# A fused decoder block in 16-bit-split fp32: another written-out order of its mixer and gate stage, and fixed places for the mixer's tiles

## Chip, cores and metric

The kernel runs on one core of a Trainium2 chip, as one launch. The metric is device time in microseconds (us), the median of three runs. The engines are TensorE (PE; its weight loads are PEld), VectorE (DVE), ScalarE (ACT), GpSimd (POOL) and SyncE (SP), which issues DMAs.

## What is computed

512 tokens and 16 prepended meta tokens, width 1024, one layer, everything in fp32. Cut to what matters:

```python
proj = rms_norm(h, norm1_g) @ w_in                      # q 512, k 128, v 128, u 512
attn = sliding_window_attention(q, k, v, ...)           # 8 heads, window 128, sinks, meta tokens
ssm  = s5_ssm(u, ...)                                   # 32 groups x 64 complex states, GLU
h    = h + concat(rms_norm(attn), rms_norm(ssm)) @ w_out
tok  = rms_norm(h, norm2_g)                             # 512 x 1024
q    = tok @ w_query                                    # 8 heads x 2 halves x 128
s1, s2 = q_half1 @ keys1, q_half2 @ keys2               # 128 keys each
v1, i1 = top_k(s1, 16); v2, i2 = top_k(s2, 16)
sc, ci = top_k(v1[:, None] + v2[None], 16)              # 16 of 256 sums
idx  = i1[ci // 16] * 128 + i2[ci % 16]                 # of 16384 experts
g    = softmax(sc)
act  = gelu(peer_u[idx] . tok) * g
h    = h + sum(act * peer_v[idx])                       # 16 experts x 8 heads per token
```

## The kernel before

Every fp32 operand of a large product is split into a high part (cast or scaled on ACT, L94 and L97) and a low part (what is left, a subtraction, L95 and L98); a product is three matmuls, high·high, low·high and high·low.

**Mixer** (`front`). Its 498 steps stand in the string `STEPS`, and the code runs them in that order, so that the string is each engine's order. `lw` loads a weight tile (L229), `lx` a pair of x tiles (L220), `sx`/`su` split them, `u0` to `u7` are the eight steps of 24 matmuls that form the 512 SSM channels (L184 to L186, into all eight PSUM banks `ps_u`); each needs the two parts of one x tile (`xh`, `xl`) and one weight tile (`w_uh`, `w_ul`). In between DVE and POOL work out the state-space constants (`tt`, L172; the blocks `bdr`, `bdi` are copied by ACT, L587). At the end the attention and SSM outputs meet in `wo`, the second norm (L971) and its transposes `nt` (L977) give `hTh` and `hTl` (L194), what all later products read.

Nine tiles of 128×2304 fp32 rotate under one tag (`b8`), and eight PSUM banks under another (`ps`): the next tile takes the place that was given out longest ago.

**Gate stage** (in `body`). Its 899 steps stand in `WSTEPS`:

- `Lq`, `Aq`, `Dq` load one of 16 query weight tiles, make its high part on ACT (L1041) and its low part (L1045), on DVE for the numbers in `QV`, else on POOL; `qm`, `qk`, `qs`, `qo` are the product (L1050 to L1052), its evacuation (L1057), the 128 key scores (L1063) and their copy to `qsc` (L1067).
- `tk` finds the 16 best keys of one head half and token tile, with MAX8, FIND_INDEX8 and MATCH_REPLACE8 on DVE (L1016 to L1024); then, per token tile n, `ca`, `tp`, `ga`, `rk`, `xe` and `oh` (one-hot work, L1137 to L1145) turn them into 16 experts per head.
- Gates, for n < 3: `go` and `gg` make one-hot rows (L1187) and weighted ones (`ggt`, L1201) on DVE, `gm` multiplies them on PE (`ps_gm`, L1217, L1218), `gc` copies the result by ACT (L1224), `gs` stores it: a dense table of gates.
- For the first 54 of 128 blocks of experts: `Lu` loads a block of `peer_u` (L1317), `Au` makes its high part `uh` on ACT (L1321), `Du` its low part `ul` (L1325), on DVE for the blocks in `UV`, else on POOL; `sm` is the block's 74 matmuls `ps_sb` with the tokens (L1333 to L1335), `so` its copy `s` by ACT (L1341).
- `rl` and `rs` gather single rows for the fourth token tile, whose experts are not done densely (L1366, L1386).

**Main loop** over 128 blocks (L1483 to L1548): gates times scores, gelu, and the products with `peer_v` (`acc`, L1543 to L1545), beside the scores of the blocks from 54 on and the rows of the fourth tile (L1393).

Of the kernel before, what the change touches and what calls it, by code (L numbers as in the profile page):

```python
# [110 lines left out]
STEPS = """
    bdz Lx4 drz Lwu3 Lwu1 ang Lwu5 Lx0 Swu3 Sx4 Lwu0 Lwu4 Swu1 sin par0 Lprm Swu0 Sx1 Lwu6 Lwq0 par1 Sx0 Swu5 Lwkv3
    Swu6 Lwkv2 par2 Lxn0 Lxm par3 sq1 par4 Lx2 rot0 rot1 Lx6 Lxn2 Sx2 co00 Lwu2 sq0 u0 Lwkv1 u1 Swkv1 Swu2 Swu4 Lwu7
    sq2 co30 rot2 Sx3 u2 u3 Sx5 wt00 wt10 bdc Swkv3 u4 sq3 u5 sq4 Lwkv0 r1 Sx6 Lwo70 rot3 Sx7 Lwq1 Swkv0 u6 Swq0 par5
    Swu7 wt01 u7 uc0 dg2 dg0 dg3 uc3 rm0 dg1 Lwq7 rm2 Swkv2 rm3 rm1 wt11 dg4 we00 co31 co01 rm4 uc1 Lwq6 kv0 we10 rot4
    rbc co11 we01 wc00 kv3 uc2 Lwq5 wc10 uo1 co10 Lwq2 uo3 rot6 rot5 us1 kv1 k0 kvc3 we11 k3 uo0 kv4 uo2 kc0 us2 co21
    wc01 q0 k1 wt20 us0 kv2 us3 wt21 Swq1 kvc0 we21 wt30 co20 wc11 kvc4 kvc1 q1 wt31 ui0 ui1 M0z kc1 we20 we31 we30
    kvc2 Swq2 x0 kc3 hmq wc21 sc20 wc20 wc31 wc30 hkq x2 hks Lwq3 Swq3 q2 sc21 hms sc00 Lwq4 x1 sc01 diz Swq6 Lwo50 q3
    Swq4 k2 sc02 Swq7 kc2 Swq5 sc03 q4 Lcst Lwo60 q5 sc10 hmx Lwo00 sc11 q6 hkx mt kd1 q7 kd0 kt sc22 qc0 qc1 sc12 qc2
    ktc sc13 hq1q hq1s qc3 hq0q y0 hq3q sc23 Lwo01 hq2q hq1x hq2s y1 yc0 y2 hq0s mtc hq3s qt1 hq2x yc1 Lwo71 qtc1 y3  # L120
    ms1 qt2 s11 s10 Lglu yc3 Swo00 yc2 hq0x hq3x msc1 qt0 gelu m11 qtc0 qt3 zt0 zt1 zt2 qtc3 zc0 qtc2 ms0 ms3 ms2 s01
    zc2 zc1 msc2 zt3 s21 m10 zc3 Lg2 sink1 msc0 s20 g0 m21 msc3 m01 s00 m00 e11 pt13 g3 sink0 Lwo20 m20 go0 s31 e10
    e00 pt01 sink2 e01 sums1 go3 g2 sums0 e21 pt02 m31 s30 pmt0 pt11 pmt1 g1 pt23 m30 pt12 Lwo30 pc13 go2 sink3 Swo60
    pt10 pc12 pc11 pc02 Lwo40 Lwo10 gs0 gq0 pmc1 e20 Swo70 pmc0 pm1 pc01 pt00 pm0 pc10 Lwo51 e31 pt32 pc00 pt21 pt20
    pc23 pv12 pt22 pt03 pc32 pc20 pv10 e30 pt31 sums3 pt30 Lwo41 pv00 sums2 pc30 pmt3 go1 pc21 pc03 pmt2 gs2 pmc3 pv02
    Swo71 pmc2 pt33 Swo01 pv01 pm3 pv11 pc22 pv03 pc31 ao0 Swo50 pm2 Lwo61 pc33 Swo40 gs1 gs3 pv30 pv20 pv31 Swo51 gq1
    pv21 Swo61 Swo41 Swo30 at0 as01 pv13 aq0 Lwo31 Swo31 o210 Swo20 ar0 Swo10 Lwo11 o110 Lh1 o211 Swo11 Lwo21 ao1 gq2
    pv22 as00 o011 pv23 gq3 ao2 o000 Swo21 gsum aq2 pv32 pv33 at1 o001 rs aq1 Lh2 oa110 Lh0 as10 ao3 o010 oa011 oa001
    as11 o111 oa210 oa010 oa000 at2 o100 nq01 ar1 as21 oa100 o101 as20 nq00 oa111 nr0 o200 o201 nx00 sh00 nt00 nx01
    at3 oa101 nq11 nq10 sh01 Lh3 ns00 nt01 aq3 o310 nr1 ar2 oa211 as31 ns01 oa201 oa310 nq21 nx10 o311 as30 nt10 ar3  # L130
    nx11 oa200 nq20 nr2 o300 oa311 oa300 nx20 o301 nt11 nt20 ns10 sh10 sh11 nq30 nx21 oa301 ns11 nt21 nq31 nr3 nx30
    nx31 ns21 sh21 ns20 nt30 nt31 sh30 sh31 sh20 ns31 ns30
# [1444 lines left out]
```

## Time and profile before

| | |
|---|---|
| median of 3 runs | 1508.9 us (1508.6 to 1509.43) |
| the profiled execution | 1501.79 us |
| its span, first to last instruction | 1499.9 us, 1.89 us around it |
| mean granted TensorE clock | 0.989 |
| PE busy | 1441.7 us, 96% |
| DVE, ACT, POOL busy | 1172.0 us (78%), 653.4 (44%), 551.9 (37%) |

The mixer takes the span's first 245 us, the gate stage goes on to about 650 us, the main loop to the end. An engine's idle time is shown with what ended it (`<-`): the engine and tile that it waited for. A granted clock of 1.00 is 2.4 GHz, 0.50 is 1.2 GHz.

### The profile page before, as it was taken

Reading aid. Unit: us, or ns where it says so; the run is one execution under the profiler, and the core shown is the slowest. Engines: PE = TensorE matmul, PEld = TensorE weight load, DVE = VectorE, ACT = ScalarE, POOL = GpSimd, SP = SyncE. Lnnn points to the kernel's source line nnn. Section 1 sums busy time; section 2 is a strip of 40 time slices with the busy share of each in tenths; the row PEclk is TensorE's granted clock in tenths of the full one; section 3 lists DMA queues with packets and bytes.
Section 4 is the critical chain, followed back from the end, with each engine's and each line's share of the span. In section 5 each row is a group of like instructions: output and inputs, shape, how many; then the busy total and the mean of one; then the engine's idle time right before and its main releaser. Section 6 shows DMA issues by size and latency. Waiting matters only on the chain. (4 is left out here: it accounts for less than half of the span.)

```text
span 1499.9 us, 22284 instructions
## 1 busy us (share of the span) xinstructions
PE 1441.7 (96%) x8062; PEld 1275.8 (85%) x8062; DVE 1172.0 (78%) x2342; ACT 653.4 (44%) x1189; POOL 551.9 (37%) x392
## 2 busy tenths in 40 slices
...
GB/s 231 84 76 79 50 96 214 95 85 104 135 222 270 262 206 242 289 291 297 330 329 309 352 331 352 328 319 337 300 335 295 345 300 332 331 314 330 311 291 139
DMA packets 161919, 372.79 MB, mean 249 GB/s; under 512 B 19968, under 2 KB 79872, under 8 KB 158608
## 3 DMA queue, kind: packets, MB, share of 16 engines
...
q10 hardware_dynamic: 576, 1.05, 0.2%
q14 instruction: 48, 0.39, 0.1%
...
## 5 line engine op out<-in xcount | busy, mean ns | idle before, releaser
L1333 PE MATMUL ps_sb<-hTh,uh 128*128 128x384 f32 x1024 | 351.9, 344 | 4.9 <-ACT s L1341 4.4
L1335 PE MATMUL ps_sb<-hTh,ul 128*128 128x384 f32 x1024 | 347.0, 339 | 7.9 <-POOL ul L1325 5.1
L1334 PE MATMUL ps_sb<-hTl,uh 128*128 128x384 f32 x1024 | 347.1, 339 | 0.0
L1543 PE MATMUL acc<-vh,ph 128*128 128x512 f32 x768 | 299.7, 390 | 1.3 <-ACT ph L94 1.3
L1544 PE MATMUL acc<-vl,ph 128*128 128x512 f32 x768 | 299.7, 390 | 0.0
L1545 PE MATMUL acc<-vh,pl 128*128 128x512 f32 x768 | 299.2, 390 | 0.0
L1366 POOL DMA_INDIRECT row_grow<-in_v_rows_dram,idx x128 | 180.7, 1412 | 249.2 <-DVE ac L1393 194.0
L1366 POOL DMA_INDIRECT row_grow<-in_u_rows_dram,idx x116 | 161.8, 1394 | 228.3 <-DVE dots L1386 190.3
L1333 PEld LDWEIGHTS ps_sb<-hTh,uh 128*128 128x128 f32 x1024 | 193.7, 189 | 10.7 <-ACT s L1341 7.0
L1335 PEld LDWEIGHTS ps_sb<-hTh,ul 128*128 128x128 f32 x1024 | 193.8, 189 | 10.5 <-POOL ul L1325 6.4
L95 DVE TENSOR_TENSOR vl<-vr,vh 128x1024 fp32r<-128x1024 f32 x128 | 156.8, 1225 | 57.2 <-ACT vh L94 52.9
L1334 PEld LDWEIGHTS ps_sb<-hTl,uh 128*128 128x128 f32 x1024 | 193.6, 189 | 2.8
L1341 ACT ACTIVATE s<-ps_sb 128x384 f32<-128x384 f32 x128 | 63.0, 492 | 275.7 <-PE ps_sb L1335 268.6
L1545 PEld LDWEIGHTS acc<-vh,pl 128*128 128x128 f32 x768 | 144.3, 188 | 31.7 <-DVE pl L95 1.2
L1543 PEld LDWEIGHTS acc<-vh,ph 128*128 128x128 f32 x768 | 144.1, 188 | 30.1 <-ACT ph L94 2.4
L1393 DVE SCALAR_TENSOR_TENSOR ac<-row_grow,dots,ac 128x1024 f32<-128x1024 f32 x128 | 164.2, 1282 | 7.0 <-DMA row_grow<-in_v_rows_dram,idx 5.0
L1544 PEld LDWEIGHTS acc<-vl,ph 128*128 128x128 f32 x768 | 144.2, 188 | 27.0
L1325 DVE TENSOR_TENSOR ul<-ur,uh 128x1024 fp32r<-128x1024 f32 x104 | 127.2, 1224 | 43.0 <-ACT uh L1321 43.0
L94 ACT CAST vh<-vr 128x1024 fp32r<-128x1024 f32 x128 | 134.0, 1047 | 42.5 <-PE acc L1545 36.9
L1321 ACT CAST uh<-ur 128x1024 fp32r<-128x1024 f32 x128 | 133.9, 1047 | 37.2 <-PE ps_sb L1334 16.6
L1386 DVE CUSTOM_DVE_ANT_0 row_grow<-row_grow,hcr 128x1024 f32<-128x1024 f32 x116 | 137.7, 1220 | 3.5 <-DMA row_grow<-in_u_rows_dram,idx 3.5
L94 ACT CAST ph<-s 128x384 fp32r<-128x384 f32 x97 | 49.8, 513 | 186.8 <-DVE s L1498 186.8
...
## 6 DMA issues: line engine op xcount, KB each, us to landing
ur<-in_uT_dram SPq DMA_DIRECT2D x128, 512.0 KB
vr<-in_v_dram SPq DMA_DIRECT2D x128, 512.0 KB
...
```

Of the source, the lines that this page charges most:

```text
L94: nc.scalar.copy(hi, src)
L95: (eng or nc.vector).tensor_tensor(lo, src, hi.bitcast(F32), op=ALU.subtract)
L1321: S.copy(hs[b], ur[b])
L1333: E.matmul(p, hi[:, k], hTh[k][:, :384], start=(k == 0), stop=False)
L1334: E.matmul(p, hi[:, k], hTl[k][:, :384], start=False, stop=False)
L1335: E.matmul(p, lo[:, k], hTh[k][:, :384], start=False, stop=(k == KD - 1))
L1366: nc.gpsimd.indirect_dma_start(out=t, out_offset=None, in_=table, in_offset=bass.IndirectOffsetOnAxis(ap=idx[:, k:k + 1], axis=0))
L1386: V.tensor_tensor_reduce(t, t, hcr, 1.0, 0.0, op0=ALU.mult, op1=ALU.add, accum_out=dots[:, k:k + 1])
L1393: V.scalar_tensor_tensor(ac3, t, dots[:, k:k + 1], ac3, op0=ALU.mult, op1=ALU.add)
L1543: E.matmul(acc[n][h], ph[:, ts], vh[:, cs], start=(b == 0), stop=False)
L1544: E.matmul(acc[n][h], ph[:, ts], vl[:, cs], start=False, stop=False)
L1545: E.matmul(acc[n][h], pl[:, ts], vh[:, cs], start=False, stop=(b == 127))
```

## The change

The two strings hold the same steps, 498 and 899; their order is another one throughout. In the mixer the rotating places become written lists: `B8AT` gives each large tile one of nine places, `PSAT` each PSUM tile one of eight banks. `Pick` keeps its one-hot tiles by half (`self.xe[w]`, `self.oh[w]`), since the steps of the two halves now may interleave. Of the low parts, `QV` gains tile 2, `UV` gains the blocks 1, 3, 9, 14, 18, 21 and 52 and loses 15, 17, 19 and 43. What PE, ACT and the DMAs compute and move is the same. In the changed file a line after about L106 stands 8 further down (9 within `Pick` and `Gates`).

```diff
-NB8 = 9
+B8AT = (
+    "012345678832505230565204517683201"
+)
+PSAT = (
+    "0123456701672301456323415077060726706261047356142730561475230173452617520342601745306125143707356174"
...
-        PP = ctx.enter_context(tc.tile_pool(name="pA", bufs=8, space=PSUM))
+        PP = ctx.enter_context(tc.tile_pool(name="pA", bufs=1, space=PSUM))
+        b8_at, ps_at = iter(B8AT), iter(PSAT)
...
-            return shaped(B8.tile([128, 2304], F32, name=name, tag="b8", bufs=NB8), shape)
+            return shaped(B8.tile([128, 2304], F32, name=name, tag=f"b8{next(b8_at)}"), shape)
...
-            return PP.tile([128, 512], F32, name=name, tag="ps")
+            return PP.tile([128, 512], F32, name=name, tag=f"ps{next(ps_at)}")
...
-        self.xe = self.tile("xe", F16, (128, 8, 16, 16))
+        self.xe[w] = self.tile("xe", F16, (128, 8, 16, 16))
...
-            self.e = self.tile("oh", F16, (128, 8, 16, 16))
+            self.oh[w] = self.tile("oh", F16, (128, 8, 16, 16))
...
-QV = {0, 7}
+QV = {0, 2, 7}
...
-UV = {0, 2, 4, 5, 6, 8, 10, 11, 15, 16, 17, 19, 20, 22, 29, 32, 36, 37, 38, 39, 40, 41, 43, 46, 47, 48, 49, 50, 51, 53}
+UV = {0, 1, 2, 3, 4, 5, 6, 8, 9, 10, 11, 14, 16, 18, 20, 21, 22, 29, 32, 36, 37, 38, 39, 40, 41, 46, 47, 48, 49, 50, 51, 52, 53}
```

Three places of the new order. **The start, on ACT** (a number behind a name tells tiles of one name apart). Before, from the third scaled weight tile on:

```order
L97 ACTIVATE w_uh_193<-w_ur_169,pk 128x512
L94 CAST xh_197<-xr_159 128x528
L94 CAST xh_211<-xr_159 128x528
L97 ACTIVATE w_uh_215<-w_ur_157,pk 128x512
L97 ACTIVATE w_uh_221<-w_ur_201,pk 128x512
L439 ACTIVATE xn_233,ss_85<-xn_233 128x1024
L94 CAST xh_278<-xr_159 128x528
L439 ACTIVATE xn_233,ss_85<-xn_233 128x1024
L97 ACTIVATE w_kvh_349<-w_kvr_323,pk 128x256 x2
L97 ACTIVATE w_uh_355<-w_ur_288,pk 128x512
L97 ACTIVATE w_uh_359<-w_ur_171,pk 128x512
```

and now, from the fifth `u` step's weight tile (w_uh_274) on:

```order
L97 ACTIVATE w_uh_274<-w_ur_165,pk 128x512
L447 ACTIVATE xm,ss_85<-xm 16x1024
L97 ACTIVATE w_uh_279<-w_ur_159,pk 128x512
L94 CAST xh_298<-xr_163 128x528
L94 CAST xh_326<-xr_163 128x528
L447 ACTIVATE xn_228,ss_85<-xn_228 128x1024
L447 ACTIVATE xn_364,ss_85<-xn_364 128x1024
L595 COPY bdr<-prm 64x16x16
L595 COPY bdi<-prm 64x16x16
L595 COPY bdr<-prm 64x16x16
L595 COPY bdi<-prm 64x16x16
L97 ACTIVATE w_uh_398<-w_ur_372,pk 128x512
```

Before, the third `u` step's weight tile (w_uh_355) stood behind two squares of the row norm (L439) and the split of a key weight tile; now the first five `u` steps' weight tiles are made ahead of the row squares, and two squares and the four copies to `bdr` and `bdi` stand ahead of the sixth (w_uh_398) and the seventh.

**The start, on SP**, which issues the loads. Before, from the second pair of x tiles on:

```order
L220 DMA xr_159<-in_xT_dram 128x1056
L229 DMA w_ur_169<-in_w_u_dram 128x512
L229 DMA w_ur_171<-in_w_u_dram 128x512
L314 DMA prm<-in_bc_dram 128x1024
L229 DMA w_ur_201<-in_w_u_dram 128x512
L229 DMA w_qr_203<-in_w_q_dram 128x512
L229 DMA w_kvr_219<-in_w_kv_dram 128x512
L229 DMA w_kvr_225<-in_w_kv_dram 128x512
L430 DMA xn_233<-in_xrow_dram 128x2x1024
L434 DMA xm<-in_xmeta_dram 16x1024
L220 DMA xr_159<-in_xT_dram 128x1056
L220 DMA xr_130<-in_xT_dram 128x1056
```

and now:

```order
L237 DMA w_ur_159<-in_w_u_dram 128x512
L237 DMA w_ur_161<-in_w_u_dram 128x512
L228 DMA xr_163<-in_xT_dram 128x1056
L237 DMA w_ur_165<-in_w_u_dram 128x512
L237 DMA w_ur_167<-in_w_u_dram 128x512
L228 DMA xr_163<-in_xT_dram 128x1056
L442 DMA xm<-in_xmeta_dram 16x1024
```

Two 256 KB weight loads more stand ahead of the pair of x tiles that the first `u` step needs (xr_163), and the third `u` step's tile (w_ur_167) is the eleventh load where it was the 20th (w_ur_288).

**The end of the gate stage, on POOL** (L1325 makes a low part; L1366 gathers rows). Before:

```order
L1325 TENSOR_TENSOR ul_6542<-ur_6359,uh_6448 128x1024
L1366 DMA row_raw<-in_u_rows_dram,idx 128x1024 x2
L1325 TENSOR_TENSOR ul_6892<-ur_6757,uh_6828 128x1024
L1366 DMA row_raw<-in_u_rows_dram,idx 128x1024
L1325 TENSOR_TENSOR ul_6941<-ur_6699,uh_6881 128x1024
L1325 TENSOR_TENSOR ul_6994<-ur_6883,uh_6939 128x1024
L1366 DMA row_raw<-in_u_rows_dram,idx 128x1024
L1325 TENSOR_TENSOR ul_7007<-ur_6924,uh_7005 128x1024
L1366 DMA row_grow<-in_u_rows_dram,idx 128x1024 x4
L1325 TENSOR_TENSOR ul_7070<-ur_7001,uh_7068 128x1024
L1366 DMA row_grow<-in_u_rows_dram,idx 128x1024 x16
```

and now (L1333 and L1374 are the same lines):

```order
L1333 TENSOR_TENSOR ul_6423<-ur_5938,uh_6395 128x1024
L1374 DMA row_raw<-in_u_rows_dram,idx 128x1024
L1333 TENSOR_TENSOR ul_6629<-ur_6406,uh_6606 128x1024
L1374 DMA row_raw<-in_u_rows_dram,idx 128x1024
L1333 TENSOR_TENSOR ul_6788<-ur_6627,uh_6786 128x1024
L1333 TENSOR_TENSOR ul_6866<-ur_6719,uh_6856 128x1024
L1374 DMA row_raw<-in_u_rows_dram,idx 128x1024 x2
L1333 TENSOR_TENSOR ul_6997<-ur_6917,uh_6931 128x1024
L1374 DMA row_raw<-in_u_rows_dram,idx 128x1024
L1374 DMA row_grow<-in_u_rows_dram,idx 128x1024
L1374 DMA row_raw<-in_u_rows_dram,idx 128x1024
L1374 DMA row_grow<-in_u_rows_dram,idx 128x1024 x19
```

Of the low parts, the blocks 21, 9, 18 and 52 have left this list, and 19, 15 and 17 have come in; the last on POOL is that of block 7, which was third from last.

## Rows read from the trace of the kernel before

**Rows 1.** Busy time of each engine in stretches of the span: the stretch in us, its length, busy us of PE, PEld, DVE, ACT and POOL with instructions in brackets, granted TensorE clock, DMA share and GB/s.

```profile
200.00:250.00 50.00, 44.69 (x217) 36.39 (x216) 29.19 (x84) 15.99 (x68) 5.30 (x8) 0.92 0.40 137
...
350.00:400.00 50.00, 43.62 (x232) 41.13 (x231) 47.49 (x245) 26.60 (x30) 16.70 (x7) 0.97 0.39 123
...
450.00:500.00 50.00, 48.01 (x378) 45.96 (x376) 49.32 (x126) 43.00 (x88) 10.21 (x4) 1.00 0.67 242
...
600.00:650.00 50.00, 47.66 (x309) 46.53 (x308) 21.95 (x24) 26.15 (x54) 20.83 (x13) 0.97 0.88 316
...
800.00:1450.00 650.00, 650.00 (x3250) 588.78 (x3250) 525.18 (x630) 227.95 (x316) 282.75 (x208) 1.00 0.92 324
```

**Rows 2.** Waits of PE over the whole span, longest in total first: line, tile, what ended the wait, us in total, times, longest.

```profile
PE ps_u L184 <- ACT xh L94: 13.1, 1, 13.1
PE ps_u L184 <- ACT w_uh L97: 6.5, 1, 6.5
PE ps_sb L1335 <- POOL ul L1325: 5.1, 4, 1.5
PE ps_sb L1333 <- ACT s L1341: 4.4, 6, 1.4
PE ps_xi L535 <- ACT WT L383: 3.0, 1, 3.0
...
PE ps_qq L1050 <- DVE hTl L194: 2.7, 1, 2.7
PE ps_ht L977 <- DVE aux L971: 2.6, 1, 2.6
PE ps_gm L1217 <- DVE ggt L1201: 2.6, 3, 1.3
```

**Rows 3.** Stretches of ten us at the start, with the columns of the first group.

```profile
10.00:20.00 10.00, 5.31 (x22) 5.01 (x23) 8.90 (x32) 3.83 (x8) 6.95 (x14) 1.00 0.89 313
...
30.00:40.00 10.00, 9.64 (x66) 9.33 (x67) 9.55 (x18) 9.30 (x20) 1.85 (x1) 0.82 0.35 103
40.00:50.00 10.00, 10.00 (x84) 9.86 (x82) 6.39 (x13) 2.13 (x6) 9.53 (x11) 1.00 0.27 83
```

**Rows 4.** PE in order of time, 12 to 48 us: start in us, us, engine, line, operation, tiles, count, and in brackets the idle time before.

```profile
15.28 0.59 PE L185 MATMUL ps_u<-xl,w_uh 128*128 128x264 f32 x1 [1.64 <-DVE xl L95]
...
29.85 0.59 PE L184 MATMUL ps_u<-xh,w_uh 128*128 128x264 f32 x1 [6.51 <-ACT w_uh L97]
```

**Rows 5.** PE in order of time, 44 to 56 us: what follows the last `u` step.

```profile
49.45 0.60 PE L457 MATMUL ps_r<-dg,ones 128*128 128x128 f32 x4
```

**Rows 6.** ACT in order of time, 0 to 42 us.

```profile
29.09 1.32 ACT L97 ACTIVATE w_uh<-w_ur,pk 128x512 fp32r<-128x512 f32 x2
...
32.41 0.40 ACT L587 COPY bdr<-prm 64x256 f32<-64x256 f32 x1
```

**Rows 7.** DVE in order of time, 5 to 42 us: of the state-space constants an undisturbed small operation, the first and the last long one of a run, and the last product on `prm`; then low parts of weight tiles.

```profile
18.79 0.17 DVE L172 TENSOR_TENSOR den<-pk 128x16 f32<-128x16 f32 x1
18.99 1.12 DVE L172 TENSOR_TENSOR den<-den,t 128x16 f32<-128x16 f32 x1
...
24.27 1.38 DVE L172 TENSOR_TENSOR t<-nr,pk 128x16 f32<-128x16 f32 x1
...
28.46 0.43 DVE L172 TENSOR_TENSOR prm<-prm 128x256 f32<-128x256 f32 x1
...
29.42 0.88 DVE L98 SCALAR_TENSOR_TENSOR w_kvl<-w_kvr,pk,w_kvh 128x256 fp32r<-128x256 f32 x2
30.21 1.41 DVE L98 SCALAR_TENSOR_TENSOR w_ul<-w_ur,pk,w_uh 128x512 fp32r<-128x512 f32 x2
```

**Rows 8.** POOL in order of time, 0 to 42 us.

```profile
17.22 1.22 POOL L172 TENSOR_TENSOR ptmp<-prm,pr 128x576 f32<-128x576 f32 x1 [1.21 <-issue]
```

**Rows 9.** Waits of DVE, 245 to 560 us.

```profile
DVE wql L1045 <- ACT wqh L1041: 24.7, 1, 24.7
...
DVE v L1016 <- ACT qsc L1067: 4.3, 5, 1.8
```

**Rows 10.** POOL in order of time, 450 to 550 us: low parts of blocks 45, 3 and 13.

```profile
455.68 3.62 POOL L1325 TENSOR_TENSOR ul<-ur,uh 128x1024 fp32r<-128x1024 f32 x1 [3.74 <-ACT uh L1321]
...
516.70 2.54 POOL L1325 TENSOR_TENSOR ul<-ur,uh 128x1024 fp32r<-128x1024 f32 x1 [11.18 <-ACT uh L1321]
541.25 2.71 POOL L1325 TENSOR_TENSOR ul<-ur,uh 128x1024 fp32r<-128x1024 f32 x1 [22.01 <-ACT uh L1321]
```

**Rows 11.** DVE in order of time, 500 to 548 us.

```profile
515.70 4.09 DVE L1201 TENSOR_TENSOR ggt<-goh,g 128x1024 f16<-128x1024 f16 x3
...
523.29 1.28 DVE L1201 TENSOR_TENSOR ggt<-goh,g 128x1024 f16<-128x1024 f16 x2
...
541.02 4.09 DVE L1201 TENSOR_TENSOR ggt<-goh,g 128x1024 f16<-128x1024 f16 x3
```

**Rows 12.** PE in order of time, 505 to 560 us.

```profile
519.84 0.22 PE L1217 MATMUL ps_gm<-ggt,goh 128*128 128x128 f16 x1 [1.12 <-DVE ggt L1201]
```

**Rows 13.** PE in order of time, 540 to 575 us.

```profile
545.16 0.23 PE L1217 MATMUL ps_gm<-ggt,goh 128*128 128x128 f16 x1 [1.27 <-DVE ggt L1201]
```

**Rows 14.** DVE in order of time, 450 to 462 us.

```profile
455.82 1.22 DVE L1325 TENSOR_TENSOR ul<-ur,uh 128x1024 fp32r<-128x1024 f32 x1
```

**Rows 15.** PE in order of time, 640 to 652 us.

```profile
644.64 0.69 PE L1335 MATMUL ps_sb<-hTh,ul 128*128 128x384 f32 x1 [1.52 <-POOL ul L1325]
```

More of the change, by code (lines that the diff above doesn't have):

```diff
@@ L105 @@
 SL = 544
-NB8 = 9
 NRW = 6
 MAGIC = 12582912.0
-STEPS = """
[L112 to L132, printed above, removed]
```

133 lines of the change are left out of this document (78 added, 55 removed).

## The prediction

> **What bounds the kernel now.** I read the stretches of the span first, then PE's waits, then for each stretch with idle PE the engines in order of time. In the stretches [rows 1] PE is busy for all 650 us of 800 to 1450 at a granted clock of 1.00: the main loop is matmuls end to end, the change leaves its code alone, and nothing is to be had there. What PE loses lies ahead of it. Of its longest waits [rows 2] two stand at the start (13.1 us for the first x tile, 6.5 for a weight tile), two at the seam between mixer and gate stage (2.6 and 2.7), 3.0 inside the mixer, and 5.1, 4.4 and 2.6 in the gate stage, for low parts from POOL, copies by ACT and gate rows from DVE. A second loss is the clock: behind a wait it is granted at half for a while, 0.82 on average in 30 to 40 us [rows 3] right behind the wait of 6.51 [rows 4], and 0.92 in 200 to 250 us, 0.97 in 350 to 400 and 600 to 650 [rows 1], stretches that all hold waits. A wait is thus dearer than its row says: 0.03 of 50 us is another 1.5 us.
>
> In the gate stage PE is not its own master. DVE is busy for 47.49 of 50 us in 350 to 400 and 49.32 in 450 to 500 [rows 1], with the searches for the best keys and the one-hot rows. From about 550 us on it is PE that DVE waits for, and DVE has half its time free (21.95 of 50 busy in 600 to 650).
>
> The sum is made against the profiled execution (1501.79 us, of which 1499.9 is span); the median is 7.1 us above it, and I carry differences over to the median unchanged.
>
> **The change, part by part.** No step is added or removed, so PE's busy time stays. The written places and the tiles by half issue no instruction; they only decide which earlier reader a tile waits for, and are counted with the order. That leaves six stretches.
>
> *Start, 0 to 50 us.* Before, the eight `u` steps end at 49.45 [rows 5]; the third waited 6.51 us [rows 4] for a tile that ACT scaled at 29.09 [rows 6], behind two row-norm squares and a pair of key tiles; its load was the 20th. Now this load is the eleventh and the first five steps' tiles are made ahead of the squares, so this wait goes. Two things take its place. Half a MB more is loaded ahead of the first pair of x tiles: at the 313 GB/s of 10 to 20 us [rows 3] that is 1.7 us later, of which the 1.64 us wait for `xl` [rows 4] takes most back, since two x tiles' low parts now stand together. And the sixth step's tile stands on ACT behind the copies to `bdr`, which need DVE's last product on `prm`. That one ended at 28.9 before [rows 7]; ahead of it now stand, by the order of the two kernels, three more x parts and one more weight part (0.70 each) and two key parts (0.44 each) [rows 7], 3.7 us, and x comes 1.7 later: it ends at about 34.3, and four copies of 0.40 and two tiles' worth of 0.66 at most [rows 6] make some 36.5. PE is through five steps (24 matmuls each; 84 matmuls in 10 us at full clock [rows 3], so 2.9 us a step) at 14.7 + 14.3 + some 2 for half clock = 31. A new wait of about 5 us stands where 6.5 stood, with its half clock behind it; what is left is about 1.5, taken as −1.5. Bounds: −6 if DVE's small operations run free of POOL (six, from 18.99 to 24.27, took 1.1 to 1.4 us instead of 0.17 [rows 7] while POOL ran six 576-wide ones, the first at 17.22 [rows 8]), +3 if they collide as before and the row squares ahead of the copies wait for their 1 MB loads as well.
>
> *Mixer, 50 to 225 us.* The longest wait is the 3.0 us of [rows 2], at the end of a long chain that the new order starts no earlier; POOL's part of the constants starts some 5 us later with DVE's. I take 0, between −3 and +3.
>
> *Seam.* PE has 5.3 us of waits there [rows 2] and a clock of 0.92 in 200 to 250 us. The second norm still ends the chain; a few more `wo` and transpose groups lie ahead of its last transposes. I take −0.5, between −5.3 (all of it) and +1.
>
> *Gate stage to 500 us.* DVE's first search begins after a wait of 24.7 us for ACT's high part of the query tile that is wanted first, and it then sat 4.3 us in five waits for scores [rows 9]. Tile 2's low part now falls into those 24.7 us, so its 1.22 us cost nothing (if that cover is gone, +1.2). The new order of `tk` has a score ready for nearly every search; I take half of the 4.3 us as gained on DVE. PE's own losses, 6.4 us idle in 350 to 400 [rows 1], are waits for POOL's low parts and ACT's copies, and there the low parts of blocks 26 and 27 still come one after the other on POOL, right ahead of the matmuls. I take −1, between −6 and +4.7 (the slower rival).
>
> *500 to 560 us.* While POOL made the low part of block 3, at 516.70 for 2.54 us, and that of block 13, at 541.25 for 2.71 [rows 10], three `ggt` on DVE that began just before took 4.09 us; two of them take 1.28 when POOL is quiet [rows 11], so three 1.9, and 2.2 us are blocked time. PE waited 1.12 and 1.27 us for just these `ggt` [rows 12, 13]. It goes both ways: where DVE's own low part (1.22) ran first, at 455.82 [rows 14], POOL's took 3.62 [rows 10]. Blocks 1 and 3 move to DVE, so two such collisions go: DVE pays 2 × 1.22 and gets back about 2 × 2.2. Block 13 stays on POOL. I take −2 (one wait of 1.1 and the share of half clock behind it), between −5 and +1.
>
> The Trainium skill (SBUF — State Buffer, "Who interferes with whom") has this as a rule: a VectorE instruction with two SBUF inputs and a GpSimd instruction that reads SBUF want the same port, and whichever starts first holds it to its end. By that rule, on which the trace agrees, the four low parts that move the other way (15, 17, 19, 43) may block DVE for up to 2.41 us each, against 4 × 1.22 us taken off it: block 43, the only one ahead of 545 us, would cost 1.2 us net and the sum be −6.3 instead of −7.5.
>
> *600 to 650 us.* PE lost 2.34 us and 0.03 of its clock [rows 1]. The last of its waits, 1.52 us at 644.64, was for POOL's low part of block 52 [rows 15]. Blocks 9, 18 and 52 go to DVE, which is idle there more than half the time and needs 1.22 us where POOL needs 2.41. POOL keeps blocks 17, 12 and 7, earlier. I take −2.5 of the 2.34 + 1.5; between −4 and 0 (the copies by ACT would then be late).
>
> Sum: −1.5 + 0 − 0.5 − 1 − 2 − 2.5 = −7.5, a median of 1501.4 us. The six bounds will not all be met at once; taken together as the root of their squares they reach some 9 us to either side.
>
> **Rivals.** *The waits only move.* PE's waits in the gate stage add up to little over 12 us in pieces of 1 us [rows 2], and behind each removed one stands the same DVE with hardly any idle time. For it: 49.32 of 50 busy. Against it: blocked time of 2.2 us goes from DVE, and behind 550 us DVE has time. It gives 1508.9, within 3 us (0.2%, about what a measurement of this kernel can tell from no change).
>
> *Slower: DVE ahead of 545 us.* What DVE gains in work before its last searches is added one to one to the end of its saturated part. Low parts 1 and 3 and query tile 2 add 3 × 1.22, block 43 takes 1.22 away, but on POOL it stands amid one-hot steps and can block one for 2.2: together +4.7, if the collisions of blocks 1 and 3 only find other victims and the start gives nothing. That is 1513.6. It decides from the point where DVE's idle time between 285 and 545 us does not fall below the 4.3 us of [rows 9]. For it: DVE's saturation. Against it: the removed collisions stand in the rows.
>
> *More.* If the new order also clears PE's 6.4 us idle in 350 to 400 us and the start's new wait is short, 6 + 4 us come on top: 1491.
>
> **How the numbers follow.** The forecast, 3 to 13 us off, I give 0.57, the larger gain 0.05: faster by over 0.2% 0.62. That the waits only move: 0.20. Slower: 0.18. The range reaches from 1492, just above the larger gain, to 1512, into the slower case; 0.05 below and about 0.1 above stay out.
>
> **What would show it.** Right: no wait of PE for a third `u` tile but a shorter one, 4 to 5 us, before the sixth, and the mixer's end within 3 us of the old place; no `ggt` group of three at 4.09 us behind block 3; no POOL low part at the end of PE's wait at 640 to 650 us; main loop unchanged at 650 of 650 busy. Wrong: the start's last step ending over 3 us earlier or later than 49 us; in 285 to 545 us more DVE blocked by POOL than before; a wait of PE in 350 to 450 us longer than any before; or a clock at half in a stretch that had it full.

## The result

| | before | changed | ratio, 95% interval |
|---|---|---|---|
| median, first measurement | 1508.88 us (4 runs) | 1493.68 us (1489.59 to 1496.84, 4 runs) | 0.9897 [0.9868, 0.9926] |
| median, measured again (changed_again) | 1504.4 us (19 runs) | 1495.71 us (1489.39 to 1498.87, 9 runs) | 0.9935 [0.9912, 0.9959] |
| span of the profiled execution | 1499.9 us | 1487.8 us | |

The change makes the kernel faster, by 15.2 us the first time and 8.7 the second; forecast were 7.5 and a range of 1492 to 1512. (The ratio is the recorded one; it is not quite the quotient of the two medians, and the two can lie 0.1% apart.) Executions of one kernel lie up to 13 us apart (the kernel before: 1499.15 to 1512.1 in 19 runs), and the cause of that turns out to be a part of the answer. So below a kernel is compared by three marks of its profiled execution as well, since the order of steps leaves the same PE work ahead of each. Both profiled executions are quick ones for their kernel (1501.79 and 1489.59 us):

| us | before | changed | difference |
|---|---|---|---|
| first query matmul (end of the mixer) | 245.75 | 238.54 | −7.2 |
| first `acc` (end of the gate stage) | 654.99 | 641.39 | −13.6 |
| start of the last matmul | 1494.85 | 1482.93 | −11.9 |

Mixer −7.2, gate stage −6.4, main loop +1.7.

The stretches of the changed kernel, with the columns of [rows 1]:

```profile
350.00:400.00 50.00, 43.40 (x234) 41.82 (x232) 49.31 (x214) 28.02 (x31) 16.43 (x7) 0.97 0.42 134
...
500.00:550.00 50.00, 50.00 (x436) 48.70 (x435) 44.31 (x56) 41.45 (x101) 5.66 (x4) 1.00 0.81 289
550.00:600.00 50.00, 50.00 (x381) 48.90 (x381) 36.66 (x38) 37.20 (x87) 15.08 (x8) 1.00 0.71 243
600.00:650.00 50.00, 42.46 (x235) 39.76 (x234) 20.32 (x27) 17.07 (x26) 13.18 (x9) 0.90 0.76 274
```

From 500 to 600 us PE is now busy for all of it, at a clock of 1.00. In 350 to 400 it idles 6.6 us where it idled 6.4 [rows 1]. In 600 to 650 it is worse: 42.46 busy and a clock of 0.90, against 47.66 and 0.97.

PE's waits over the span, as in [rows 2]. First two of the kernel before that are not shown there, then the changed kernel:

```profile
PE ps_y L635 <- DMA M<-kp: 2.4, 1, 2.4
...
PE ps_w L376 <- DVE wt L172: 1.1, 1, 1.1
```

```profile
PE ps_u L192 <- ACT w_uh L97: 17.6, 2, 14.3
PE acc L1551 <- ACT ph L94: 7.0, 3, 5.7
PE ps_sb L1341 <- ACT s L1349: 5.0, 4, 3.2
PE ps_qq L1058 <- DVE hTl L202: 4.3, 1, 4.3
PE ps_ht L985 <- DVE aux L979: 3.0, 1, 3.0
...
PE ps_k L604 <- POOL vi L180: 1.7, 1, 1.7
PE ps_sb L1343 <- POOL ul L1333: 1.4, 2, 1.0
```

The waits for `WT` (3.0), `M` (2.4) and `wt` (1.1) are gone, and 1.7 for `vi` from POOL has come, with 0.7 for `mw` from DVE. For low parts from POOL PE waits 1.4 us in place of 5.1. At the seam of mixer and gate stage it waits 3.0 and 4.3 in place of 2.6 and 2.7. New is the wait of 5.7 us at the first `acc`.

PE at the start, then behind the `u` steps, to set beside [rows 4] and [rows 5] (a view each):

```profile
14.26 0.59 PE L192 MATMUL ps_u<-xh,w_uh 128*128 128x264 f32 x1 [14.26 <-ACT w_uh L97]
...
35.25 0.39 PE L192 MATMUL ps_u<-xh,w_uh 128*128 128x264 f32 x1 [3.35 <-ACT w_uh L97]
```

```profile
47.20 0.38 PE L465 MATMUL ps_r<-dg,ones 128*128 128x128 f32 x2
```

ACT there, beside [rows 6]: the sixth and seventh tiles, right behind the last of the copies to `bdr` and `bdi`.

```profile
34.05 0.40 ACT L595 COPY bdi<-prm 64x256 f32<-64x256 f32 x1
34.47 1.33 ACT L97 ACTIVATE w_uh<-w_ur,pk 128x512 fp32r<-128x512 f32 x2
```

The wait that stood before the third step now stands before the sixth, 3.35 us long, and the steps end at 47.20 in place of 49.45.

DVE, 500 to 560 us, beside [rows 11]: the first group of three `ggt`.

```profile
522.12 1.90 DVE L1210 TENSOR_TENSOR ggt<-goh,g 128x1024 f16<-128x1024 f16 x3
```

No group of three is at 4.09 there any more (the others take 1.89 and 1.90).

### The profile page after: what moved, and what is told of

Same layout as the page of the kernel before. It is cut to its first block, busy times and chain, and to the rows that moved or that the text cites. A ratio compares the mean times of both kernels' runs of the same rounds, so it can differ in the third digit from the quotient of the medians.

```text
span 1487.8 us, 22281 instructions
## 1 busy us (share of the span) xinstructions
PE 1434.8 (96%) x8062; PEld 1272.3 (86%) x8062; DVE 1178.0 (79%) x2346; ACT 652.8 (44%) x1189; POOL 540.9 (36%) x388
## 4 chain that ended last, share of the span: by engine, by line
PE 44%; DVE 3%; issue 2%; ACT 1%; DMA 0%; ACTq 0%; DVEq 0%
PE acc L1553 8%; PE acc L1552 8%; PE acc L1551 8%; PE ps_sb L1341 7%; PE ps_sb L1343 7%; PE ps_sb L1342 7%; DVE ac L1401 2%; ACT ph L94 1%; DVE s L1506 1%; DMA ur<-in_uT_dram 0%; DVE vl L95 0%; DVE sr L1506 0%; ACT vh L94 0%; DVE o L1555 0%; DVE ul L1333 0%
## 5 line engine op out<-in xcount | busy, mean ns | idle before, releaser
L1374 POOL DMA_INDIRECT row_grow<-in_v_rows_dram,idx x128 | 179.1, 1399 | 250.8 <-DVE ac L1401 194.1
L1374 POOL DMA_INDIRECT row_grow<-in_u_rows_dram,idx x116 | 160.8, 1386 | 236.5 <-DVE dots L1394 194.5
L95 DVE TENSOR_TENSOR vl<-vr,vh 128x1024 fp32r<-128x1024 f32 x128 | 156.7, 1225 | 50.0 <-ACT vh L94 45.4
L1333 DVE TENSOR_TENSOR ul<-ur,uh 128x1024 fp32r<-128x1024 f32 x107 | 130.9, 1224 | 50.6 <-ACT uh L1329 47.3
```

What stands on the lines that cost most here:

```text
L95: (eng or nc.vector).tensor_tensor(lo, src, hi.bitcast(F32), op=ALU.subtract)
L1374: nc.gpsimd.indirect_dma_start(out=t, out_offset=None, in_=table, in_offset=bass.IndirectOffsetOnAxis(ap=idx[:, k:k + 1], axis=0))
```

## The new wait at the seam to the main loop

PE, then SP, then DVE of the changed kernel around 640 us (`gates<-gst` stores gates, `gc<-gates` loads them for the main loop, `vr` is a block of `peer_v`):

```profile
641.39 0.79 PE L1551 MATMUL acc<-vh,ph 128*128 128x512 f32 x1 [5.74 <-ACT ph L94]
```

```profile
613.59 1.61 SPq L1237 DMA_DIRECT2D gates<-gst  x2
625.25 0.33 SPq L1491 DMA_DIRECT2D vr<-in_v_dram  x1
625.77 0.37 SPq L1496 DMA_DIRECT2D gc<-gates  x1
```

```profile
640.24 0.56 DVE L1506 SCALAR_TENSOR_TENSOR s<-gc,s 128x384 f32<-128x384 f32 x1 [3.95 <-DMA gc<-gates]
```

and SP of the kernel before, the same stores and the same load:

```profile
626.76 0.86 SPq L1228 DMA_DIRECT2D gates<-gst  x1
...
635.64 0.38 SPq L1488 DMA_DIRECT2D gc<-gates  x1
```

The stores of the last gates are issued until 615.20, their load at 625.77, and DVE has them at 640.24: 25.0 us from the one to the other. (Before, it was 21.6 us, from 627.62 by way of 635.64 to 649.27; DVE waited 6.9 us for them there, and PE did not.) Only then can `s`, `ph` and the first `acc` follow. The last gate matmul starts at 610.56, and between it and the first `acc` PE has the matmuls of five blocks, some 21 us (24 matmuls each, not 74 as said in the description of the gate stage, at 0.175 us from one start to the next); before, seven blocks followed, some 29.5 us. The new order leaves PE less other work behind the last gates than their way through DRAM takes. Behind the wait the clock is down as well: 0.70 in the first 5 us from the first `acc` on, where the kernel before has 1.00, which makes 1.5 of the 1.7 us that the main loop is longer.

## Experiments

All times of profiles are of one execution; the lines in the profiles of some kernels are shifted by the edit. Marks and medians of all runs (gate stage: from the first query matmul to the first `acc`). Each ratio is to runs of the kernel before beside it, with a median of 1508.88 us for changed, 1506.86 for the four kernels from new_mixer to new_order_old_places, 1506.63 for b3_on_dve, start_early_tiles, gates_first and rows8, and 1504.4 for the other four:

| kernel | first query matmul | gate stage | span | median us | ratio to before, 95% interval |
|---|---|---|---|---|---|
| before | 245.75 | 409.2 | 1499.9 | 1504.4 to 1508.9 | |
| changed | 238.54 | 402.9 | 1487.8 | 1493.68 | 0.9897 [0.9868, 0.9926] |
| changed_again | 238.02 | 404.8 | 1489.0 | 1495.71 | 0.9935 [0.9912, 0.9959] |
| new_mixer | 237.45 | 408.6 | 1490.6 | 1495.85 | 0.9937 [0.9915, 0.9959] |
| new_gate | 255.99 | 406.4 | 1509.1 | 1508.15 | 1.0009 [0.9990, 1.0029] |
| old_order_new_places | 253.32 | 429.4 | 1527.1 | 1528.43 | 1.0155 [1.0127, 1.0183] |
| new_order_old_places | 241.95 | 414.1 | 1502.1 | 1506.87 | 1.0003 [0.9984, 1.0022] |
| b3_on_dve | 246.66 | 413.0 | 1504.1 | 1509.87 | 1.0033 [1.0011, 1.0054] |
| k2_earlier | 243.18 | 409.8 | 1497.8 | 1500.34 | 0.9971 [0.9954, 0.9988] |
| start_early_tiles | 235.60 | 403.3 | 1486.4 | 1490.18 | 0.9898 [0.9861, 0.9936] |
| gates_first | 242.84 | 404.6 | 1494.6 | 1493.09 | 0.9907 [0.9871, 0.9943] |
| rows8 | 242.34 | 401.6 | 1491.1 | 1492.81 | 0.9907 [0.9872, 0.9943] |
| last_gates_earlier | 238.35 | 403.8 | 1487.0 | 1492.99 | 0.9928 [0.9903, 0.9954] |
| best | 240.05 | 400.5 | 1487.6 | 1489.20 | 0.9899 [0.9875, 0.9923] |

**The two halves: new_mixer and new_gate.** Each has one half of the change (for new_gate the mixer's string, rotating places and buffer counts are those of before).

```diff
 # new_mixer: of the changed kernel, WSTEPS, QV and UV as before
 # new_gate: of the changed kernel, STEPS, the "b8" and "ps" tiles as before
-        PP = ctx.enter_context(tc.tile_pool(name="pA", bufs=1, space=PSUM))
+        PP = ctx.enter_context(tc.tile_pool(name="pA", bufs=8, space=PSUM))
```

> The changed mixer (order and written places) with the gate stage as before. Theory: the two halves of the change add up; the mixer's is what it took between the span's start and the first query matmul, 245.75 to 238.54, so the span falls by about 7 us, from 1499.9 to some 1493, with the first query matmul at 238 to 239 and the waits of the gate stage as before the change. Rival: the gate stage is bound by DVE, whose work only begins earlier with PE's, and half or more of the 7 us comes back there: span 1496 or more.

> The changed gate stage (order, tiles by half, QV and UV) with the mixer as before. Theory: first query matmul at 245 to 246 as before; between the last query matmul and the last gate matmul some 8 us less are lost, between the last gate matmul and the first acc some 4 us more; span about 1495 (1499.9 - 4.7). Rival: the loss at the seam to the main loop only stands there because PE came early; with the mixer late it is not there and the span falls by 8 or more.

The mixer alone gives 0.9937, all that changed_again has, and none of it comes back in the gate stage (408.6 against 409.2): theory held, rival out. The gate stage alone gives nothing in the median that can be told from no change. In the profiles it does two things of its own, under either mixer: PE's idle time of 3.0 us in 500 to 550 us (3.8 in new_mixer) falls to 0 in the changed kernel and 0.8 in new_gate, and the wait at the first `acc` comes (5.4 us in new_gate, with a late mixer, so that new_gate's rival is out too). But its expected span of 1495 is far off, at 1509.1.

In new_gate's execution the first query matmul came at 255.99, though its mixer is that of before, which had 245.75. Six of these ten us stand right at the seam. PE there, before and in new_gate:

```profile
245.75 0.76 PE L1050 MATMUL ps_qq<-hTh,wqh 128*128 128x512 f32 x1 [2.67 <-DVE hTl L194]
```

```profile
255.99 0.80 PE L1057 MATMUL ps_qq<-hTh,wqh 128*128 128x512 f32 x1 [8.95 <-ACT wqh L1048]
```

The new `WSTEPS` loads query tile 0, the first that is wanted, as the third tile (`Lq4 Lq9 Lq0`), where it was the first (`Lq0 Lq4`). Behind the old mixer ACT waits 6.30 us for that load, at 254.89. So 6.3 us of new_gate's first mark are the new gate stage's, and its 406.4 us leave them out. The other four are there by the last transposes (245.72 against 241.31), and they show in the stretches of new_gate behind the wait for `M`:

```profile
110.00:120.00 10.00, 7.54 (x38) 5.70 (x38) 9.68 (x21) 5.41 (x9) 0.00 (x0) 0.88 0.76 129
120.00:130.00 10.00, 10.00 (x48) 6.79 (x46) 7.93 (x18) 1.02 (x3) 6.43 (x4) 0.50 0.30 107
130.00:140.00 10.00, 10.00 (x78) 7.45 (x77) 1.47 (x3) 1.78 (x3) 0.23 (x1) 0.94 0.00 0
140.00:150.00 10.00, 9.65 (x80) 8.19 (x79) 5.93 (x23) 6.37 (x16) 0.00 (x0) 0.92 0.26 80
150.00:160.00 10.00, 10.00 (x43) 5.66 (x43) 6.71 (x44) 8.02 (x33) 0.00 (x0) 0.91 0.00 1
```

and of before:

```profile
110.00:120.00 10.00, 7.58 (x39) 5.69 (x39) 9.68 (x21) 5.41 (x9) 0.00 (x0) 0.94 0.82 139
120.00:130.00 10.00, 10.00 (x74) 6.95 (x72) 9.56 (x22) 1.02 (x3) 5.34 (x4) 0.88 0.28 107
```

From 130 us on the clock is at 1.00 there. The wait is the same (2.46 and 2.42 us). Behind it half clock takes 1.8 us' worth (0.06 + 0.12 of ten us) in one execution, and 8.5 in the other (0.12 + 0.50 + 0.06 + 0.08 + 0.09 of ten us). Two more profiles with the old mixer have 0.84 (b3_on_dve) and 0.50 (old_order_new_places) in 120 to 130 us; old_order_new_places loses 12.0 us' worth from 110 to 150, and its last transposes come 7.9 us later than those of the kernel before. The Trainium skill (TensorE: Matmul & The Clock Gate, "What's actually happening") says of a kernel's first matmuls that the number at half clock differs from run to run; here the same holds behind a wait in mid-kernel, with these numbers beside it.

**One wait of the old mixer: k2_earlier.**

```diff
-    ... q3 Swq4 k2 sc02 Swq7 kc2 ...
+    ... k2 kc2 q3 Swq4 sc02 Swq7 ...
```

> The kernel before with one move in the mixer's string: the product k2 and its copy kc2, which the loads of M wait for, stand ahead of the product q3 instead of behind it (12 matmuls, 2.9 us). Theory (the changed mixer gains by the waits it removes, and by the half clock that follows them for a time that differs from execution to execution): PE's wait of 2.4 us for M in 110 to 120 us goes or falls below 0.5, the stretch of 110 to 150 us keeps a clock of 0.98 or more also in executions that had it at 0.5 in 120 to 130, the first query matmul comes at 240 to 243 us, and the median falls by 3 to 7 us. Rival (waits of the mixer only move, since its chain to the second norm is bound by DVE and ACT): the first query matmul stays at 245 or later and the median within 2 us of the kernel before.

PE's waits from 50 to 230 us, and the clock behind the one for `M`:

```profile
PE ps_k L574 <- DVE sc L152: 1.5, 1, 1.5
PE ps_y L615 <- DMA M<-kp: 1.2, 1, 1.2
PE ps_xi L515 <- ACT WT L363: 1.0, 1, 1.0
```

```profile
110.00:120.00 10.00, 8.81 (x52) 6.55 (x50) 9.66 (x22) 5.88 (x10) 0.00 (x0) 1.00 0.74 135
120.00:130.00 10.00, 10.00 (x80) 7.30 (x80) 9.65 (x23) 1.31 (x4) 4.56 (x3) 1.00 0.30 107
```

The wait for `M` is halved, not gone, 1.5 us for `k` is new, and the clock stays at 1.00. The first query matmul gains 2.6 us on the profile of before, but the median 4.1, and its twelve runs lie between 1499.22 and 1503.61 where 19 of the kernel before lie between 1499.15 and 1512.1: the upper part of the spread is gone, while the fastest runs of the two are alike. In the median the theory held and the rival is out; of the theory's smaller marks the wait (1.2, not below 0.5) and the first query matmul (243.18, not within 240 to 243) just miss. So a wait in the mixer costs what its row says, and in some executions more behind it: 4.4 us by the last transposes in new_gate, 7.9 in old_order_new_places. The changed mixer has this too, behind its wait of 1.7 us at 90 us: the profiles of new_order_old_places, gates_first and rows8 have a clock of 0.66 in 90 to 100 us, where changed, changed_again and new_mixer have 1.00, and their first query matmul comes 3 to 5 us later.

**Order or engine: old_order_new_places and new_order_old_places.**

```diff
-QV = {0, 7}
-UV = {0, 2, 4, 5, 6, 8, 10, 11, 15, 16, 17, 19, 20, ...}
+QV = {0, 2, 7}
+UV = {0, 1, 2, 3, 4, 5, 6, 8, 9, 10, 11, 14, 16, 18, 20, 21, ...}
```

(the second kernel: the other way round, in the changed one)

> The kernel before, with the changed QV and UV alone: the same order of steps, seven low parts of expert blocks and one of the queries on DVE in place of POOL, four on POOL in place of DVE. Theory (it is the engine of the low parts that brought the gain between 450 and 600 us, since POOL's low parts block DVE): no gate rows of three at 4.09 us behind block 3; PE loses 3 to 6 us less in 400 to 600 and 2 us less in 600 to 650; span 1493 to 1496. Rival (it is the order): within 2 us of 1499.9, or slower, since 15, 17, 19 and 43 now stand on POOL right ahead of their matmuls.

> The changed kernel with QV and UV as before. Theory (engine of the low parts): 4 to 8 us of the gain go, span 1492 to 1496, with gate rows on DVE at 2.7 us and more while POOL makes low parts of blocks 1, 3, 14. Rival (order): within 2 us of 1487.8.

Both theories fall in their simple form. The new engines under the old order cost 22 us in the median, the old engines under the new order 11 to 13 (against the changed kernel's two medians). PE's waits in 360 to 690 us, of the kernel before and then of old_order_new_places:

```profile
PE ps_sb L1335 <- DVE ul L1325: 2.1, 3, 1.3
```

```profile
PE ps_sb L1335 <- DVE ul L1325: 19.7, 7, 5.1
PE ps_sb L1335 <- POOL ul L1325: 3.5, 3, 1.4
```

and DVE's for PE in 420 to 690 us, in the same order:

```profile
DVE goh L1187 <- PE ps_gm L1218: 20.3, 14, 4.0
```

```profile
DVE goh L1187 <- PE ps_gm L1218: 45.4, 22, 6.7
```

POOL's part in PE's waits fell, from 5.1 us [rows 2] to 3.5, but PE now waits 19.7 us for low parts from DVE, where the low part stands in line behind `goh` instructions that wait for PE themselves (45.4 us in 22 waits). So the rival's "slower" came, and not for the reason it gave. In new_order_old_places PE waits 6.5 us for low parts from DVE and 3.9 for POOL's (2.3 and 1.4 in the changed kernel), and its gate stage is 9 to 11 us longer.

**One low part: b3_on_dve.**

```diff
-UV = {0, 2, 4, ...
+UV = {0, 2, 3, 4, ...
```

> The kernel before, with block 3 alone added to UV: its low part is made by DVE (1.22 us) and no longer by POOL (2.54 us at 516.70). Theory (the port is held to the end of an instruction): the three gate rows of 515.70 take 1.9 us in place of 4.09, PE's wait of 1.12 us at 519.84 goes, span 1 to 2 us shorter. Rival: DVE is the bound there, pays 1.22 us and PE waits elsewhere: span within 0.5 us of 1499.9.

DVE, 514 to 530 us, and PE there:

```profile
516.81 1.89 DVE L1201 TENSOR_TENSOR ggt<-goh,g 128x1024 f16<-128x1024 f16 x3
520.85 2.36 DVE L1187 TENSOR_TENSOR goh<-itx,iT 128x2048 f16<-128x2048 f16 x2 [2.15 <-PE ps_gm L1218]
...
524.33 1.22 DVE L1325 TENSOR_TENSOR ul<-ur,uh 128x1024 fp32r<-128x1024 f32 x1
```

```profile
525.61 0.44 PE L1335 MATMUL ps_sb<-hTh,ul 128*128 128x384 f32 x1 [3.53 <-DVE ul L1325]
```

The three `ggt` take 1.89 us in place of 4.09 [rows 11], and the wait of 1.12 us [rows 12] is gone: the collision was what the rows said. The rule of the Trainium skill weighed in the prediction (SBUF — State Buffer, "Who interferes with whom") agrees with that. But block 3's low part comes at 524.33 only, behind two `goh` for which DVE sat 2.15 us until PE freed their place, and PE waits 3.53 us for it. Slower, 1.0033 [1.0011, 1.0054]: neither theory's number, though the rival's PE waiting elsewhere is what is seen.

**The start: start_early_tiles.**

```diff
-    ... Lxn0 par4 Lwu5 sq3 sq0 bdc par5 rot2 Lwkv3 Lwq6 Swu5 u2 Swu6 Swq0 ...
+    ... Lxn0 Lwu5 Swu6 Swu5 par4 sq3 sq0 bdc par5 rot2 Lwkv3 Lwq6 u2 Swq0 ...
```

> The changed kernel; in the mixer's string the splits of the sixth and seventh u step's weight tiles stand ahead of the two row squares and the four copies to bdr and bdi. Theory (ACT's order makes the wait): PE's wait of 3.35 us at 35.25 falls below 1 us, the u steps end at 43 to 45 in place of 47.20, and the first query matmul comes 2 to 3 us earlier; span 1485 to 1486. Rival (the mixer has a later bound, DVE and POOL's constants): the u steps end earlier, but PE waits for the copies to bdr or for the row statistics after them, and the first query matmul stays within 0.7 us of 238.54.

```profile
38.08 0.59 PE L192 MATMUL ps_u<-xh,w_uh 128*128 128x264 f32 x1 [2.99 <-ACT xh L94]
41.14 0.59 PE L193 MATMUL ps_u<-xl,w_uh 128*128 128x264 f32 x1 [2.48 <-DVE xl L95]
```

The wait moved one step on: the seventh waits 2.99 us for its x tile, which stands behind the copies as before the edit, and 2.48 for its low part. The steps end at 48.23 (47.07 in the changed kernel, the start of the last matmul in both), not earlier. That the first query matmul still comes 2.9 us sooner is not from there: the wait of 1.7 us for `vi` is down to 0.3 (PE is busy for 9.68 of 10 us in 90 to 100, 8.29 before the edit), and 1.7 us' worth of half clock that the changed kernel's profiled execution had in 180 to 200 us (0.85 and 0.98) is not in this one, nor in changed_again's. The median can't be told from the changed kernel's.

**The seam: gates_first, rows8, last_gates_earlier.**

```diff
 # gates_first
-            v_load(0)
             g_blocks(0)
+            v_load(0)
 # rows8: ROWS=12 to ROWS=8, steps rl8 to rl11 and rs8 to rs11 taken out
 # last_gates_earlier
-    ... so17 sm9 gc2.14.1 gc2.7.1 gm2.6.1 rs8 Au18 gm2.6.0 gc2.6.0 so9 Du7 sm7 Du18 gc2.6.1 so7 Lu51 gs2.7 ... Au53 gs2.3 rl11
+    ... so17 gc2.14.1 gc2.7.1 gm2.6.1 gm2.6.0 gs2.7 gc2.6.1 gc2.6.0 gs2.3 sm9 rs8 Au18 so9 Du7 sm7 Du18 so7 Lu51 ... Au53 rl11
```

> The changed kernel; ahead of the main loop SP issues the load of the first gates before the load of the first block of peer_v, which waits for a raw buffer until 625.25. Theory A (the load of the gates is issued too late, at 625.77, since it is queued behind the other): it is issued up to 10 us earlier, when the last gate stores are done, and PE's wait of 5.7 us at the first acc falls to 2 or less: span 1483 to 1485. Theory B (the load is slow, 14.4 us for 1.5 MB, since gathers of rows share the DMA engines): issue moves by 2 us at most and the wait stays over 3.5 us: span 1486 to 1488.

> The changed kernel with 8 in place of 12 row gathers made ahead of the main loop; the other four are made within it. Theory B (gathers in the way of the first gates): the gates land in 6 to 9 us in place of 14.4, PE's wait at the first acc falls below 2 us, span 1483 to 1485. Theory A (issued too late): the wait stays at 4 us or more unless the load of peer_v gets its buffer earlier. In either case the four gathers cost nothing in the main loop, where PE is never idle.

> The changed kernel; at the end of the gate stage's string the last two products of gates (gm2.6), their copies and the last two stores stand ahead of the block products sm9, sm7 and of the load of block 51. Theory (the seam waits for the last gates on their way through DRAM, some 9 us until the stores are done and 11 to 15 us for the load, and PE has too little work to cover it): 8.4 us more of matmuls stand behind the last gate product, the wait of 5.7 us at the first acc goes or falls below 1, and the span is 4 to 6 us shorter than the changed kernel's in an execution with the same mixer. Rival (PE then waits for the gate copies and for low parts instead): a wait of 3 us or more at ps_gm or ps_sb in 600 to 640 us, and no gain over 1.5 us.

SP of gates_first, SP and DVE of rows8, PE of last_gates_earlier:

```profile
620.20 1.60 SPq L1237 DMA_DIRECT2D gates<-gst  x2
630.81 0.37 SPq L1496 DMA_DIRECT2D gc<-gates  x1
```

```profile
616.89 2.61 SPq L1237 DMA_DIRECT2D gates<-gst  x2
...
625.83 0.37 SPq L1496 DMA_DIRECT2D gc<-gates  x1
```

```profile
636.68 0.56 DVE L1506 SCALAR_TENSOR_TENSOR s<-gc,s 128x384 f32<-128x384 f32 x1 [6.46 <-DMA gc<-gates]
637.16 1.22 DVE L1333 TENSOR_TENSOR ul<-ur,uh 128x1024 fp32r<-128x1024 f32 x1
```

```profile
642.14 0.50 PE L1503 MATMUL acc<-vh,ph 128*128 128x512 f32 x1 [2.55 <-ACT ph L94]
```

Issuing the load first moves it little: it goes out 9.0 us behind the last stores (630.81 − 621.8), in place of 10.6 (625.77 − 615.2), and the wait was 6.7 us; theory A falls. In rows8 the load goes out 6.3 us behind the stores (625.83 − 619.5) and takes 10.9 us, in place of 14.5; from the stores to the use of the gates it is 17.2 us, and 19.0 in the kernel with this edit and others (best, below), against 23.2 to 29.8 in the seven profiles of the new gate order with all 12 gathers. That bears theory B out in kind, though the load's own time does not go by the gathers alone (13.4 us in best, 13.6 before the change, with four gathers issued beside it in each, as in rows8). No wait is left at the first `acc`, but 3.6 us stand just ahead of it for the low part of block 53, queued on DVE behind the wait for the gates (637.16), and the span is 1491.1 where 1483 to 1485 was expected; 3.8 us of that lie in the mixer, whose first query matmul came at 242.34. That leaving out the four gathers costs nothing elsewhere, as was expected, is not seen: the main loop of rows8 and of best takes 842.15 us, 2.3 more than new_mixer's, which has no wait at the first `acc` either. Whether the gathers are the cause is not shown.

With the last gates ahead of sm9 PE has one block more behind them (4.2 us; the 8.4 that I expected also counted sm7, which stood behind them already), and the wait falls to 2.55; the span is 0.8 to 2.0 us shorter, not 4 to 6. Against the two profiles of the changed kernel (402.9 and 404.8) none of the three moves the gate stage by more than their own difference can hide, rows8 excepted by 1.3 us; none of the medians can be told from the changed kernel's.

**All three edits: best.**

> The changed kernel with three edits together: the early sixth and seventh tiles at the start, 8 row gathers ahead of the main loop instead of 12, and the last gates ahead of sm9 and sm7. If the seam's wait and the gathers' share in it are what the runs before say, no wait of PE over 2 us stands at the first acc, and the time falls by 4 to 9 us against the changed kernel. If low parts on DVE behind the load of the first gates are the next bound, a wait of 2 to 4 us for a low part stays and the gain is 1 to 4 us.

No wait over 0.8 us at the first `acc`; 2.8 us for a low part are left, as in the second case, though the median gains as in the first. The gate stage is 2.4 to 4.3 us shorter than the changed kernel's, the median 6.5 us below changed_again's on the same chip; the intervals, [0.9875, 0.9923] and [0.9912, 0.9959], just overlap, so that best beats the kernel before is shown and that it beats the changed one is likely, not shown.

> The changed kernel once more, on the same chip and beside the same runs of the kernel before, as the mark for the two kernels above. Expected: 1490 to 1497, with the first query matmul between 237 and 243 us depending on how long the clock stays at half behind the wait at 90 us; the waits of PE in the same places and of the same length, within 0.5 us.

Same places, with 7.7 us at the first `acc` in place of 5.7, more than the 0.5 allowed.

## Why the prediction was right, and where its sum was not

The sign and the range were right. Against the second measurement's 8.7 us the sum of 7.5 looks close as well, but by luck: it gave the mixer 0 and the gate stage 5.5 us, and the runs show the other way round. new_mixer alone has the whole gain of changed_again, and new_gate none. By the prediction's own terms, in the profiled executions:

- *Start, −1.5*: −2.25. Right as put, with the new wait before the sixth step at 35.25 (3.35 us; about 5 at 36 was foretold).
- *Mixer, 0, between −3 and +3*: this is the step that failed. From the end of the `u` steps to the waits of the seam it took 6.3 us less (189.2 and 182.9 us). I looked at the longest wait alone and called its chain unmoved. The waits for `WT`, `M` and `wt` (3.0 + 2.4 + 1.1) went and 1.7 + 0.7 came; PE idled 8.3 us there before and 3.7 after. Half clock is no part of this in these two executions: 1.8 us' worth behind `M` went, and 1.7 came in 180 to 200 us. In other executions it is: the profile read was one that had little half clock behind `M`. It was 7.1 us under the median, and I carried that over as a constant instead of asking where it was.
- *Seam, −0.5*: +1.3. Its waits are 2 us longer.
- *Gate stage to 500 us, −1*: PE idled 9.6 us in 350 to 500 before and 8.3 after, the size that was forecast, by other waits than I named. Those for POOL's low parts fell from 3.6 to 0.4 us, and 3.19 for a copy by ACT and 2.04 for a low part from DVE came. DVE's waits for scores, 4.3 us, of which I took half as gained, add up to 10.7 in 245 to 560 us.
- *500 to 560 us, −2*: 500 to 600 us lost 3.7 us of idle and 1.5 of clock, all of it gone: the place was right, the size half. The reason was not enough: one collision less does not pay by itself, as b3_on_dve shows; the low part must also stand in DVE's line where nothing ahead of it waits for PE, and that is the order's work. My price of a moved low part (1.22 us on, 2.2 off) lacked it.
- *600 to 650 us, −2.5, between −4 and 0*: wrong, outside its bounds. The waits for POOL's low parts went (1.4 us is left in the whole span), but the gates' way through DRAM, covered before, is no longer: +5.7 us of wait, and half clock behind it, which reaches into the main loop (its +1.7 us). I had named the copies by ACT as what is late next; it was the load of the gates.

The gate stage's terms thus come to −6.4 us in the profile, 1.7 of which the main loop gives back. Beside new_mixer's profile the changed kernel's spans are 1.6 and 2.8 us shorter; in the medians that is not shown.

Of its own signs, the one on the mixer's end failed (7.2 us, not within 3), and two of those for "wrong" came: a wait of PE in 350 to 450 us longer than any before (3.19 us at 360.25, 1.43 before), and a clock below full where it had been full (0.85 in 180 to 190 us, 0.70 behind the first `acc`).

Of the rivals, the slower one's moved low parts do cost 22 us under the old order, but not by its mechanism: DVE is not fuller there but emptier (37.69 of 50 us busy in 500 to 550, 46.48 before), since it waits for PE. In the change itself the order avoids it. What the rule of the port would take for block 43 can't be seen: PE's loss in 350 to 500 us fell. Open is why the gate stage's own gain is 4 to 6 us behind the new mixer and 2.8 behind the old: of the difference new_gate has a wait of 6.3 us for one low part from DVE where the changed kernel has 2.0, but what makes it longer is not shown.
